# Sigmoids written as tanh, gate products in halves, head shares added one by one, and another order of work within a tick

## The chip, the cores and the metric

The kernel runs on one core of one Trainium2 chip. Its time is device microseconds of one launch; the median of three runs before the change is 3244.39 us (3243.58 to 3248.15). The engines are called TensorE (PE, with PEld for its weight loads), VectorE (DVE), ScalarE (ACT), GpSimd (POOL) and SyncE (SP, which issues most DMAs).

## The reference

A sequence of 512 tokens of width 1024 goes through two blocks, all in float32. The first block has two layers; each is a feed-forward network (width 2816), a mixer, a cross attention over 256 memory tokens, and a second feed-forward network. Layer 0 has the even mixer (eight heads of banded attention with sinks, eight heads of stick-breaking attention), layer 1 the odd mixer (16 heads of 64, three dilated bands in one softmax). The second block has a recurrent unit and a sparse attention side by side, then a feed-forward network:

```python
r = sigmoid(xb @ w_a + b_a); i = sigmoid(xb @ w_x + b_x)
log_a = -8 * r * softplus(-lam); a = exp(log_a)
u = sqrt(-expm1(2 * log_a)) * (i * x)          # h[t] = a[t] * h[t-1] + u[t]
merged = sigmoid(g_a) * y_a + sigmoid(g_b) * y_b
mix = merged @ w_o
```

`y_a` is the recurrent unit's output through a projection, `y_b` that of the attention (16 heads, 4 key-value heads, keys outside a query's 128 best by index scores are masked out).

## The kernel before, in words

Each float32 product is made of three matmuls of float32r parts: every operand is split into a high part (a rounded copy, ScalarE) and a low part (a subtraction, VectorE). Activations lie with features on the partitions, eight tiles of 128 x 512. `feat` (matmuls at L312 to L314) makes one 128 x 512 block of features in one PSUM bank by 24 matmuls; `tok_bank` (L785 to L787) makes token-major projections, two token tiles of 256 columns to a bank, 48 matmuls a bank. `weights` loads a weight block by SyncE's queue and splits it (L306 ScalarE, L307 VectorE). PSUM has 8 banks; SBUF temporaries are 36 slots of 128 x 512.

An attention pair is two heads (`heads`, which drives two `head` generators). Scores are 24 matmuls of 64 rows into six banks (L920); VectorE adds the bias and takes the maximum, which frees the bank (L944); ScalarE makes the exp and its sums (L953); GpSimd normalizes (L963); TensorE transposes the probabilities into three banks for each head (L974), which `evac` copies out in two parts (L848 ScalarE, L849 VectorE); eight matmuls multiply them with the values into one bank (L983, L984). The values' high and low parts sit side by side, so rows 0 to 63 and 64 to 127 of that bank are two shares of one head's result. `finish_heads` adds the shares of both heads when both are there (L993 and L994 copy, L995 and L996 add) and splits the sum (L514, L515).

What runs when is written as ticks. `drive` takes a list of ticks, each with fills (projections, output units, gates) and tasks (heads). All are generators, and every `yield` hands over to the next tick. In each tick `drive` starts the fills, then steps the generators that are under way, oldest first, then starts the tasks. This gives the order in which instructions are issued, which the compiler's scheduler takes as priority: on each engine an instruction of lower priority goes ahead where it reckons that the one of higher priority is not ready. The result is a fixed order on each engine. A pair takes five ticks: scores, maxima and exp of both heads; normalizing the first; transposes of the first and normalizing the second; values of the first and transposes of the second; values of the second. A new pair starts every second tick.

The odd mixer fills its ticks with query, key and value projections of four heads (`proj`, whose banks are held from the first half of its matmuls to the scaling three ticks later) and with the first output units. The second block's attention has query projections in every fourth tick and, in odd ticks, `gate_b`: a `feat` product, a scaling, a sigmoid and a store to DRAM. `merge_b` loads that back, multiplies it with the attention's projection, adds the recurrent side, and splits. Before this, the recurrent stage runs eight `rnn_block`s (two gate sigmoids, tanh, exp, square, square root, gelu, a scan) beside the index scores and the steps that find the 128 best keys on VectorE (L1542, L1543), and eight `merge_a` units with the other gate. ScalarE loads a table before a function that the loaded one lacks; the compiler places these loads, and in the profile they carry the line of the activation that follows.

Of the kernel before, what the change touches and what calls it, by code (L numbers as in the profile page):

```python
# [10 lines left out]
F32 = mybir.dt.float32  # L11
# [3 lines left out]
OP = mybir.AluOpType  # L15
# [159 lines left out]
class Net:  # L175
# [413 lines left out]
    def drive(self, ticks):  # L589
# [7 lines left out]
        def step(g, into):  # L597
            try:
                next(g)
                into.append(g)  # L600
            except StopIteration:
                pass

        i = 0
        while i < len(ticks) or act:
            fills, tasks = ticks[i] if i < len(ticks) else ((), ())
            i += 1
            new = []
            for f in fills:
                start(f, new)  # L610
            old = []
            for g in act:
                step(g, old)
            for f in tasks:
                start(f, new)
            act = old + new
# [286 lines left out]
    def heads(self, lay, q, k, biases, values, pair, sinks=(None, None)):  # L903
# [18 lines left out]
        one, two = (self.head(lay, order, sb[x], biases[x], values[x], pair, sinks[x]) for x in range(2))  # L922
# [4 lines left out]
        yield  # L927
        next(one)
        next(two)
        yield  # L930
# [5 lines left out]
    def head(self, lay, order, sb, bias, v, pair, sink):  # L936
# [43 lines left out]
        pair.append(po)  # L980
# [4 lines left out]
        self.put(ts)  # L985

    def finish_heads(self, one, two):


        nc = self.nc  # L990
# [152 lines left out]
    def stick(self, q, k, r0, v, pair):  # L1143
# [47 lines left out]
        pair.append(po)  # L1191
# [4 lines left out]
        self.put(s)  # L1196


    def odd_mixer(self, rms, w, wout):
# [37 lines left out]
        self.drive(ticks)  # L1237
# [313 lines left out]
    def rnn_consts(self):  # L1551
# [29 lines left out]
        v.tensor_scalar(self.c8, p, 8.0, None, OP.mult)  # L1581
        v.tensor_scalar(self.nc8, p, -8.0, None, OP.mult)
# [20 lines left out]
    def rnn_block(self, b, rms, w, gw, YH, YL):  # L1603
# [16 lines left out]
        for z, (o, bias) in enumerate(((r, "rg_b_a_2"), (i, "rg_b_x_2"))):  # L1620
# [16 lines left out]
        nc.scalar.activation(m, m, AF.Sqrt)  # L1637
# [167 lines left out]
    def second(self, out):  # L1805
# [28 lines left out]
        def merge_a(b):  # L1834
# [3 lines left out]
            nc.scalar.activation(t, t, AF.Sigmoid)  # L1838
# [3 lines left out]
            def finish(b, pa):  # L1842
                nc.vector.tensor_mul(t, t, pa)
# [208 lines left out]
```

## Time and profile before

| | before |
|---|---|
| median of 3 runs | 3244.39 us (3243.58 to 3248.15) |
| profiled execution | 3245.68 us, span 3243.9 us |
| TensorE, weight load | busy 3132.0 us (97%), 2819.2 us (87%) |
| VectorE | 2264.3 us (70%) |
| ScalarE | 1629.8 us (50%) |
| GpSimd | 358.0 us (11%) |
| mean granted clock of TensorE | 0.984 |
| the chain that ended last | PE 77%, DVE 12%, ACT 5%, issue 2%, DMA 2%, POOL 1% |

The span runs from the first to the last instruction on the core, and the time of the execution includes what lies around it. Busy time is the union of an engine's instructions; waiting, branching and issuing DMAs are not counted. The chain is followed back from the last instruction, at each step to what released it. In order of time the stages are: feed-forward, even mixer (about 350 to 626 us), cross attention, feed-forward twice, odd mixer (about 1490 to 1760 us), cross attention, feed-forward, then the second block from about 2300 us: the recurrent stage to about 2575, attention to about 2771, merging and output projection, feed-forward.

### The profile page before, as it was taken

To read this page: it belongs to the slowest core of one execution; us is meant where nothing else is said; L and a number is where in the kernel's file an instruction comes from. 1 tells how busy PE (TensorE), PEld (TensorE's weight loads), DVE (VectorE), ACT (ScalarE), POOL (GpSimd) and SP (SyncE) were. 2 spreads that over 40 slices of the span, in tenths; PEclk is the share of its full clock that TensorE was granted. 3 is DMA by queue.
4 is the path that set the end of the run, shared out by engine and by line. 5 is a ranking of instruction groups with operands and counts; after the bars stand their busy time and mean duration, and the time that the engine had idled before them with its cause. 6 is when DMAs were issued, how large, how long until landed. Compare 5 with 4: busy or idle time off the path is not lost.

```text
span 3243.9 us, 50967 instructions
## 1 busy us (share of the span) xinstructions
PE 3132.0 (97%) x20420; PEld 2819.2 (87%) x20420; DVE 2264.3 (70%) x3416; ACT 1629.8 (50%) x2711; POOL 358.0 (11%) x543
## 2 busy tenths in 40 slices
PE   8999999999999999999999999999999998989998
PEld 7999887798999999999887989999876887789997
DVE  8877566656777697775557557777689455478675
ACT  6544455655444364434556555443486277354444
POOL 1000123201000010001122010000222132210001
PEclk9999998999999999999999999999999999989999
DMA  4322211322233223322223322332312321513321
GB/s 158 109 97 85 94 50 56 121 96 84 93 101 98 96 95 111 100 76 88 85 72 111 117 79 75 111 101 76 105 60 91 104 79 47 168 53 105 105 91 65
DMA packets 104335, 300.81 MB, mean 93 GB/s; under 512 B 13857, under 2 KB 17441, under 8 KB 104097
## 3 DMA queue, kind: packets, MB, share of 16 engines
q1 hardware_dynamic: 94464, 287.74, 27.3%
q10 hardware_dynamic: 9632, 9.80, 1.0%
q8 instruction: 160, 2.62, 0.3%
q14 instruction: 79, 0.64, 0.1%
HBM read 291.21 MB, written 6.29 MB: 92 GB/s over the span
## 4 chain that ended last, share of the span: by engine, by line
PE 77%; DVE 12%; ACT 5%; issue 2%; DMA 2%; POOL 1%; ACTq 0%; SPq 0%; DVEq 0%; POOLq 0%
PE bank L312 19%; PE bank L313 18%; PE bank L314 18%; PE bank L787 4%; PE bank L785 4%; PE bank L786 4%; DVE wlo L307 2%; ACT whi L306 1%; PE bank L1765 1%; PE bank L1766 1%; PE bank L1767 1%; DVE wlo L428 1%; DVE slot L515 1%; DVE gl L578 1%; PE bank L974 1%
## 5 line engine op out<-in xcount | busy, mean ns | idle before, releaser
L312 PE MATMUL bank<-slot,whi 128*128 128x256 f32 (+1 forms) x2768 | 910.0, 330 | 16.7 <-ACT slot L514 9.6
L313 PE MATMUL bank<-slot,whi 128*128 128x256 f32 (+1 forms) x2768 | 911.8, 330 | 3.5 <-DVE slot L515 3.5
L314 PE MATMUL bank<-slot,wlo 128*128 128x256 f32 (+1 forms) x2768 | 911.1, 329 | 0.0
L427 ACT CAST whi<-fq 128x1024 fp32r<-128x1024 f32 x350 | 365.7, 1048 | 504.4 <-PE bank L313 409.7
L306 ACT CAST whi<-raw 128x1024 fp32r<-128x1024 f32 (+3 forms) x363 | 345.5, 954 | 521.3 <-PE bank L313 295.3
L312 PEld LDWEIGHTS bank<-slot,whi 128*128 128x128 f32 x2768 | 521.2, 188 | 70.5 <-ACT slot L514 12.3
L313 PEld LDWEIGHTS bank<-slot,whi 128*128 128x128 f32 x2768 | 521.8, 188 | 57.9 <-DVE slot L515 7.1
L314 PEld LDWEIGHTS bank<-slot,wlo 128*128 128x128 f32 x2768 | 523.0, 189 | 50.9
L307 DVE TENSOR_TENSOR wlo<-raw,whi 128x1024 fp32r<-128x1024 f32 (+3 forms) x363 | 411.8, 1136 | 218.8 <-ACT whi L306 218.0
L312 PE MATMUL bank<-gh,whi 128*128 128x256 f32 (+1 forms) x1712 | 538.8, 316 | 13.1 <-ACT whi L352 8.7
L314 PE MATMUL bank<-gh,wlo 128*128 128x256 f32 (+1 forms) x1712 | 534.7, 313 | 3.8 <-DVE wlo L353 2.5
L313 PE MATMUL bank<-gl,whi 128*128 128x256 f32 (+1 forms) x1712 | 535.5, 313 | 1.0 <-DVE gl L578 1.0
L428 DVE TENSOR_TENSOR wlo<-fq,whi 128x1024 fp32r<-128x1024 f32 x350 | 426.2, 1221 | 147.9 <-ACT whi L427 147.4
L312 PEld LDWEIGHTS bank<-gh,whi 128*128 128x128 f32 x1712 | 325.1, 190 | 39.8 <-ACT whi L352 9.4
L314 PEld LDWEIGHTS bank<-gh,wlo 128*128 128x128 f32 x1712 | 325.8, 190 | 26.0 <-DVE wlo L353 3.4
L313 PEld LDWEIGHTS bank<-gl,whi 128*128 128x128 f32 x1712 | 325.7, 190 | 24.0 <-DVE gl L578 2.3
L785 PE MATMUL bank<-whi,gh 128*128 128x256 f32 (+1 forms) x1056 | 303.7, 288 | 2.7 <-DVE slot L852 2.7
L787 PE MATMUL bank<-whi,gl 128*128 128x256 f32 (+1 forms) x1056 | 301.4, 286 | 1.5 <-DVE gl L578 1.5
L786 PE MATMUL bank<-wlo,gh 128*128 128x256 f32 (+1 forms) x1056 | 301.2, 285 | 1.1 <-DVE wlo L307 0.9
L172 POOL TENSOR_TENSOR sqacc<-sqacc,slot 128x512 f32<-128x512 f32 x62 | 100.5, 1621 | 1550.1 <-ACT slot L168 1549.2
L785 PEld LDWEIGHTS bank<-whi,gh 128*128 128x128 f32 x1056 | 202.5, 192 | 4.1 <-DVE slot L852 3.2
L786 PEld LDWEIGHTS bank<-wlo,gh 128*128 128x128 f32 x1056 | 202.6, 192 | 2.4 <-DVE wlo L307 2.0
(319 smaller groups left out, 4612.4 us busy)
## 6 DMA issues: line engine op xcount, KB each, us to landing
fq<-in_ffn_w_gu_dram SPq DMA_DIRECT2D x160, 512.0 KB, 3.3
raw<-in_ffn_w_down_dram SPq DMA_DIRECT2D x96, 384.0 KB, 3.1
raw<-in_w_in_dram SPq DMA_DIRECT2D x46, 512.0 KB, 3.4
raw<-in_xa_w_kv_dram SPq DMA_DIRECT2D x32, 512.0 KB, 3.5
raw<-in_od_w_in_dram SPq DMA_DIRECT2D x24, 512.0 KB, 3.3
raw<-in_w_ffn_down_dram SPq DMA_DIRECT2D x22, 512.0 KB, 3.5
fq<-in_w_ffn_gate_dram SPq DMA_DIRECT2D x40, 256.0 KB, 2.8
fq<-in_w_ffn_up_dram SPq DMA_DIRECT2D x40, 256.0 KB, 3.3
```

The lines of the kernel that those rows point to most:

```text
L172: self.net.nc.gpsimd.tensor_add(self.parts[0], self.parts[0], sq)
L306: nc.scalar.copy(hi[:, :n], raw[:, :n])
L307: nc.vector.tensor_sub(lo[:, :n], raw[:, :n], hi[:, :n].bitcast(F32))
L312: mm(ps, wh, xh, start=start, stop=False, **k)
L313: mm(ps, wh, xl, start=False, stop=False, **k)
L314: mm(ps, wl, xh, start=False, stop=stop, **k)
L427: self.nc.scalar.copy(hi[:, :n], t[:, :n])
L428: self.nc.vector.tensor_sub(lo[:, :n], t[:, :n], hi[:, :n].bitcast(F32))
L515: nc.vector.tensor_sub(lo, src, hi.bitcast(F32))
L785: mm(o, XH[k][:, t], wh, start=first, stop=False, skip_group_check=True)
L786: mm(o, XH[k][:, t], wl, start=False, stop=False, skip_group_check=True)
L787: mm(o, XL[k][:, t], wh, start=False, stop=last, skip_group_check=True)
```

## The change

Four things change. Sigmoids in the second block become tanh, by sigmoid(x) = (1 + tanh(x/2)) / 2, with the halves moved into constants and scales of instructions nearby; the product of input gate and convolution thereby goes from GpSimd to VectorE. `gate_b` gives way after half of its matmuls, and starts in even ticks. A head's shares are added right after its value matmuls, in attention pairs and in the stick-breaking heads. And in the odd mixer and the second block's attention `drive` goes through a tick in another order: first the steps under way that are not marked, then the tasks (scores), then the fills, last the marked steps. `heads` marks the steps that begin with transposes of the first head and with values of the first and transposes of the second.

```diff
-    def drive(self, ticks):
+    def drive(self, ticks, heads_first=False):
...
         def step(g, into):
             try:
-                next(g)
-                into.append(g)
+                into.append((g, next(g)))
             except StopIteration:
                 pass
...
-            new = []
-            for f in fills:
-                start(f, new)
-            old = []
-            for g in act:
-                step(g, old)
+            old, new = [], []
+            if not heads_first:
+                for f in fills:
+                    start(f, new)
+            for g, late in act:
+                if not (late and heads_first):
+                    step(g, old)
             for f in tasks:
                 start(f, new)
+            if heads_first:
+                for f in fills:
+                    start(f, new)
+                for g, late in act:
+                    if late:
+                        step(g, old)
             act = old + new
...
         next(one)
         next(two)
         yield
         next(one)
-        yield
+        yield True
         next(one)
         next(two)
-        yield
+        yield True
         next(one, None)
         next(two)
         yield
         next(two, None)
...
         po = self.bank()
-        pair.append(po)
...
         self.put(ts)
+        if x == 0:
+            pair.append(self.get())
+        self.add_halves(pair[0].f, po, x)
+
+    def add_halves(self, o, po, x):
+        here, there = slice(64 * x, 64 * x + 64), slice(64 - 64 * x, 128 - 64 * x)
+        self.nc.scalar.copy(o[here, :], po[there, :])
+        self.nc.vector.tensor_add(o[here, :], po[here, :], o[here, :])
...
-    def finish_heads(self, one, two):
-        t, h, l = self.get(3)
-        lo, hi = slice(0, 64), slice(64, 128)
-        nc.scalar.copy(t.f[lo, :], one[hi, :])
-        nc.scalar.copy(t.f[hi, :], two[lo, :])
-        nc.vector.tensor_add(t.f[lo, :], one[lo, :], t.f[lo, :])
-        nc.vector.tensor_add(t.f[hi, :], two[hi, :], t.f[hi, :])
+    def finish_heads(self, t):
+        h, l = self.get(2)
         self.split(h.r, l.r, t.f)
...
-        self.drive(ticks)
+        self.drive(ticks, True)
...
-            nc.scalar.activation(o, pg, AF.Sigmoid, bias=self.col(bias, b))
-        nc.gpsimd.tensor_mul(i, i, xc.f)
-        nc.scalar.activation(m, r, AF.Tanh, scale=self.c8[:, b:b + 1])
-        nc.scalar.activation(r, r, AF.Exp, scale=self.nc8[:, b:b + 1])
+            nc.scalar.activation(o, pg, AF.Tanh, bias=self.hb[z][:, b:b + 1], scale=0.5)
+        c8, nc8 = self.c8[:, b:b + 1], self.nc8[:, b:b + 1]
+        v.scalar_tensor_tensor(i, i, 1.0, xc.f, OP.add, OP.mult)
+        nc.scalar.activation(m, r, AF.Tanh, scale=c8, bias=c8)
+        nc.scalar.activation(r, r, AF.Exp, scale=nc8, bias=nc8)
...
-        nc.scalar.activation(m, m, AF.Sqrt)
+        nc.scalar.activation(m, m, AF.Sqrt, scale=0.25)
...
-            nc.scalar.activation(t, t, AF.Sigmoid)
+            nc.scalar.activation(t, t, AF.Tanh, scale=0.5)
...
-                nc.vector.tensor_mul(t, t, pa)
+                nc.vector.scalar_tensor_tensor(t, t, 1.0, pa, OP.add, OP.mult)
...
         def gate_b(b):
-            pg = self.feat(w[:, 5192 + b * P:5192 + (b + 1) * P], self.GH, self.GL)
+            wh, wl = self.weights(w[:, 5192 + b * P:5192 + (b + 1) * P], ND, P)
+            pg = self.bank()
+            for k in range(ND):
+                if k == ND // 2:
+                    yield
+                self.mm3(pg, wh[:, k, :], wl[:, k, :], self.GH[k], self.GL[k], k == 0, k == ND - 1)
             t = self.scratch()
             nc.vector.tensor_mul(t, pg, rms.R)
-            nc.scalar.activation(t, t, AF.Sigmoid)
+            nc.scalar.activation(t, t, AF.Tanh, scale=0.5)
...
-                self.split(h.r, l.r, t.f)
+                nc.scalar.mul(h.r, t.f, 0.5)
+                nc.vector.scalar_tensor_tensor(l.r, t.f, 0.5, h.r.bitcast(F32), OP.mult, OP.subtract)
...
-            x = [q(h // 4 + 1)] if h % 4 == 0 and h < 12 else [G(h // 2)] if h % 2 else []
-            ticks.append((x, [] if h % 2 else [H(h // 2)]))
-        self.drive(ticks + [([B(0)], []), ([B(1)], [])])
+            x = [q(h // 4 + 1)] if h % 4 == 0 and h < 12 else []
+            ticks.append((x + ([] if h % 2 else [G(h // 2)]), [] if h % 2 else [H(h // 2)]))
+        self.drive(ticks + [([B(0)], []), ([B(1)], [])], True)
```

Left out above: the same call of `add_halves` at the end of `stick`, and in `rnn_consts` the factors 8 and -8, which become 4 and -4, and the two gate biases times 0.5 (`hb`, 128 x 8 each).

## Rows read from the trace of the kernel before

**Rows 1.** The page's head: span, then TensorE's busy us, share, instructions.
```profile
span 3243.9 us, 50967 instructions
PE 3132.0 (97%) x20420; PEld 2819.2 (87%) x20420; DVE 2264.3 (70%) x3416; ACT 1629.8 (50%) x2711; POOL 358.0 (11%) x543
```

**Rows 2.** Windows: length, busy (instructions) of PE, PEld, DVE, ACT, POOL; PEclk, DMA, GB/s.
```profile
350.00:626.00 276.00, 264.10 (x1560) 224.71 (x1559) 177.93 (x330) 157.14 (x321) 66.62 (x110) 0.96 0.23 78
1561.00:1755.00 194.00, 176.56 (x1272) 161.34 (x1272) 117.14 (x294) 103.84 (x258) 40.85 (x100) 0.96 0.21 66
2300.00:2575.00 275.00, 262.92 (x1310) 215.32 (x1308) 205.03 (x355) 157.85 (x209) 57.00 (x80) 0.98 0.28 91
2600.00:2771.00 171.00, 154.11 (x989) 133.96 (x987) 99.74 (x260) 118.33 (x256) 49.25 (x100) 0.96 0.19 63
...
2695.00:2702.00 7.00, 6.56 (x39) 6.46 (x40) 3.60 (x6) 3.67 (x8) 0.76 (x3) 0.76 0.20 76
...
1563.00:1575.00 12.00, 9.00 (x50) 8.43 (x49) 7.11 (x25) 5.55 (x20) 5.68 (x15) 0.72 0.38 133
```

**Rows 3.** Waits of TensorE, 2575 to 2800 us: total us, times, longest.
```profile
PE bank L983 <- ACT slot L848: 11.8, 4, 4.0
PE bank L920 <- DVE slot L849: 4.5, 8, 1.2
```

**Rows 4.** Timeline of ScalarE from 2692.78 us: start, us, instruction.
```profile
2692.78 0.19 ACT L953 ACTIVATION_READ_ACCUMULATOR slot<-slot,nm 128x1 f32 x1
2692.99 1.28 ACT L1918 ACT_TABLE_LOAD   x1
...
2694.82 1.33 ACT L848 CAST slot<-bank 128x512 fp32r<-128x512 f32 x3
```

**Rows 5.** Timeline of TensorE at the same place; idle time and releaser in brackets.
```profile
2691.69 1.28 PE L974 MATMUL bank<-ident,slot 128*128 128x128 f32 x10
2695.44 0.51 PE L983 MATMUL bank<-slot,vv 128*128 128x512 f32 x1 [2.47 <-ACT slot L848]
```

**Rows 6.** Groups by line, ScalarE, 2575 to 2771 us: busy, mean ns, idle before.
```profile
L953 ACT ACT_TABLE_LOAD x8 | 10.3, 1283 | 10.3 <-DVE nm L947 10.3
L1918 ACT ACT_TABLE_LOAD x8 | 10.3, 1283 | 0.1
```

**Rows 7.** Waits of TensorE, 1490 to 1760 us.
```profile
PE bank L920 <- DVE mx L944: 4.6, 2, 2.9
PE bank L920 <- DVE slot L849: 3.6, 3, 1.5
...
PE bank L312 <- ACT slot L514: 1.4, 1, 1.4
```

**Rows 8.** Timeline of TensorE in the odd mixer, at a later pair's scores.
```profile
1610.77 1.32 PE L920 MATMUL bank<-slot,slot 64*128 64x512 f32 x6
1613.22 2.63 PE L920 MATMUL bank<-slot,slot 64*128 64x384 f32 x18 [1.14 <-DVE slot L849]
```

**Rows 9.** Timeline of ScalarE and of VectorE at the end of a pair, odd mixer.
```profile
1745.60 0.58 ACT L994 COPY slot<-bank 64x512 f32<-64x512 f32 x1 [1.15 <-PE bank L984]
...
1746.21 0.69 DVE L996 TENSOR_TENSOR slot<-bank,slot 64x512 f32<-64x512 f32 x1 [0.89 <-ACT slot L994]
```

**Rows 10.** Waits of TensorE, 350 to 626 us.
```profile
PE bank L312 <- ACT slot L514: 2.8, 2, 1.8
```

**Rows 11.** Recurrent stage: a wait of TensorE, a window, two groups by line.
```profile
PE bank L312 <- POOL slot L512: 6.4, 3, 3.2
...
2450.00:2475.00 25.00, 24.32 (x103) 19.04 (x103) 25.00 (x49) 22.18 (x26) 9.38 (x7) 1.00 0.24 71
...
L1635 DVE SCALAR_TENSOR_TENSOR rn<-slot,rn 128x512 f32<-128x512 f32 x8 | 5.4, 680 | 0.0
...
L1628 ACT ACT_TABLE_LOAD x8 | 10.3, 1283 | 0.1
```

More of the change, by code (lines that the diff above doesn't have):

```diff
@@ L921, in heads @@
                        skip_group_check=True)
-        one, two = (self.head(lay, order, sb[x], biases[x], values[x], pair, sinks[x]) for x in range(2))
+        one, two = (self.head(lay, order, sb[x], biases[x], values[x], pair, sinks[x], x) for x in range(2))
         next(one)
@@ L934, in heads, with head @@
         next(two, None)
-    def head(self, lay, order, sb, bias, v, pair, sink):
+    def head(self, lay, order, sb, bias, v, pair, sink, x):
         nc = self.nc
@@ L985, in head @@
         self.put(ts)
-    def finish_heads(self, one, two):
-        nc = self.nc
-        t, h, l = self.get(3)
-        lo, hi = slice(0, 64), slice(64, 128)
-        nc.scalar.copy(t.f[lo, :], one[hi, :])
-        nc.scalar.copy(t.f[hi, :], two[lo, :])
-        nc.vector.tensor_add(t.f[lo, :], one[lo, :], t.f[lo, :])
-        nc.vector.tensor_add(t.f[hi, :], two[hi, :], t.f[hi, :])
+        if x == 0:
[7 more added lines that the diff above has]
+        h, l = self.get(2)
         self.split(h.r, l.r, t.f)
@@ L1190, in stick @@
         po = self.bank()
-        pair.append(po)
         for j, (b, off, q0, w) in enumerate(K):
@@ L1196, in stick @@
         self.put(s)
+        if r0 == 0:
+            pair.append(self.get())
+        self.add_halves(pair[0].f, po, r0 // 64)
     def odd_mixer(self, rms, w, wout):
@@ L1580, in rnn_consts @@
         self.nc8 = m
-        v.tensor_scalar(self.c8, p, 8.0, None, OP.mult)
-        v.tensor_scalar(self.nc8, p, -8.0, None, OP.mult)
+        v.tensor_scalar(self.c8, p, 4.0, None, OP.mult)
+        v.tensor_scalar(self.nc8, p, -4.0, None, OP.mult)
+        self.hb = []
+        for t, name in ((e, "rg_b_a_2"), (l, "rg_b_x_2")):
+            v.tensor_scalar(t, self.pv[:, ROWS[name][0]:ROWS[name][0] + n], 0.5, None, OP.mult)
+            self.hb.append(t)
     def gate_weights(self):
@@ L1619, in rnn_block @@
         r, i, m = t1[:, 0:512], t1[:, 512:1024], t1[:, 1024:1536]
-        for z, (o, bias) in enumerate(((r, "rg_b_a_2"), (i, "rg_b_x_2"))):
+        for z, o in enumerate((r, i)):
             wh, wl = gw[z]
@@ L1926, in finish @@
             def finish(b, pa):
-                nc.vector.tensor_mul(t.f, t.f, pa)
+                nc.vector.scalar_tensor_tensor(t.f, t.f, 1.0, pa, OP.add, OP.mult)
                 nc.gpsimd.tensor_add(t.f, t.f, m.f)
                 h, l = self.get(2)
-                self.split(h.r, l.r, t.f)
+                nc.scalar.mul(h.r, t.f, 0.5)
+                nc.vector.scalar_tensor_tensor(l.r, t.f, 0.5, h.r.bitcast(F32), OP.mult, OP.subtract)
                 self.put(t, m)
```

## The prediction

> **What bounds the kernel now.** I read the page's head first: TensorE is busy 97% of the span [rows 1]. A change that removes no matmul can give back only TensorE's idle time and the time it spends at the lower of its two clock levels (1.2 against 2.4 GHz). So the second view is busy time by stage [rows 2]: of 276 us of the even mixer TensorE idles 11.9, of 194 us of the odd mixer 17.4, of 275 us of the recurrent stage 12.1, and of 171 us of the second block's attention 16.9. The granted clock in the same rows turns into lost time by (1 - clock) x length: 0.96 in both attention stages is 7.8 us (odd) and 6.8 us (second). Everything the change can win lies in these sums, some 49 us in the two attention stages.
>
> Third, what ends the idle time. In the second block's attention it is nearly two waits: the probability-times-value matmuls for ScalarE's copy of the transposed probabilities (11.8 us in 4 waits), and the scores for VectorE's half of the same eviction, that is, for PSUM banks (4.5 us in 8) [rows 3]. In the odd mixer the scores again wait for banks, held by the maxima (4.6 us in 2) or by an eviction (3.6 in 3) [rows 7].
>
> **The change part by part.** All sums are against the profiled execution, 3245.7 us (span 3243.9, 1.8 around it); the median of the runs shown is 3244.4, 1.3 lower, which I take off at the end.
>
> *Sigmoid to tanh in the second block's attention.* The four long waits have one picture: the last exp ends at 2692.97, a table load of 1.28 us for the gate's sigmoid starts at 2692.99, then the sigmoid runs, and only then the three copies at 2694.82 [rows 4]; TensorE's transposes end at 2692.97 and the next matmul starts at 2695.44, 2.47 us idle [rows 5]. There are 8 loads at the sigmoid and 8 at the exp that follows [rows 6]; the exp's load lies on the way from scores to transposes, which has at least a tick of other work beside it, so only the sigmoid's, right before copies that TensorE waits for, counts. If tanh needs no load beside exp, each wait loses 1.28 us: 4 x 1.28 = 5.1 us. The bounds are 0 (tanh evicts exp's table as sigmoid does) and 5.1. I take 5.1: in the recurrent block the tanh follows the sigmoid without a load of its own in all 8 blocks, while sigmoid, exp, square root and gelu each have one (8 at the exp, and rows like it with 7, 8 and 8) [rows 11], so tanh is the one function there that never causes a load.
> That row doesn't show tanh and exp in one table, though. The Trainium skill (ScalarE: Activation LUTs, "Table sets: the hidden batching unit") states it: the set whose main function is exp also holds tanh. By that the 5.1 stands; no row here can show it. The same page of the Trainium skill ("What ACT_TABLE_LOAD costs") prices a switch at about 2.66 us, a 1.28 us load and a drain of 1.38 us. The row differs: the load starts 0.02 us after the exp's last piece, and nothing but the 1.28 us is lost. By the Trainium skill's price four switches would be 10.6 us and the time some 5.5 us lower than mine; the measurement decides.
>
> *Scores first, transposes last, gates in halves (second block).* Of the 11.8 us, 6.7 are left. They arise where the second head's transposes are followed at once by the products that need their eviction. Now half a gate product (12 of 24 matmuls) lies in each tick, and a query projection's second half and the next pair's scores are at hand. No row shows the new order; bounds are 0 and all 6.7, and I take half, 3.4, as the new order still puts that second product right behind the transposes, at the head of the next tick. The scores' wait of 4.5 us: scores now follow that product and not the first head's transposes. Bounds 0 and 4.5, half is 2.2. Splitting the gate costs no matmul; it holds one bank and one weight buffer a tick longer. Clock: around one of the long waits the granted clock is 0.76 over 7 us, 1.7 us lost [rows 2], a quarter of the stage's 6.8, so I put the other three quarters at the other three waits. Bounds 0 and 6.8, half is 3.4. Stage: 5.1 + 3.4 + 2.2 + 3.4 = 14.1 us less.
>
> *The same order in the odd mixer.* Projections keep their two banks over several ticks there. The scores' waits are 8.2 us [rows 7]; 2.9 of these belong to the first pair, which has no older pair to be put before, so its order stays. A later one shows the mechanism: six score matmuls start on free banks at 1610.77, the other 18 at 1613.22, 1.14 us of it idle [rows 8]. In the new order the scores follow the other head's transposes, with the same three banks to be drained, but with all fills behind them in the tick. Bounds 0 and 5.3; half is 2.7. Clock: 7.8 us, of which 3.4 lie beside the first pair's wait (0.72 over 12 us [rows 2]); of the other 4.4 half, 2.2.
>
> *Shares added at once.* The number of copies and adds is unchanged, 64 x 512 each, but at the end of a pair one copy (0.58 us) and one add (0.69) [rows 9] are already done: the chain to the split is 1.27 shorter. It ends a wait in the odd mixer (1.4 us, one [rows 7]), which falls by 1.3, and two in the even mixer (1.8 and 1.0 us [rows 10]), which fall by 1.3 and 1.0. Bounds 0 and 3.6; the full 3.6 is taken, because the wait is directly on this chain. The bank of the first head also comes free a tick earlier; I price that at nothing, since even-mixer waits aren't on banks. Odd mixer: 2.7 + 2.2 + 1.3 = 6.2; even mixer 2.3.
>
> *Recurrent block.* ScalarE loses about one load in four per block (tanh after gelu or exp), some 10 us; the longest waits there don't end on it but on GpSimd's split at the end of a block's chain (6.4 us in 3) [rows 11], behind a VectorE that is busy 25.00 of 25 us [rows 11]. And VectorE gets the product of input gate and convolution from GpSimd, 8 x 0.68 = 5.4 us by a like instruction [rows 11]. If a third of the blocks fall in the saturated stretch, it is some 2 us later there, against a load of 1.28 less ahead of the last square root. Bounds: 6.4 gained, 5.4 lost; I take 0. If VectorE's cover of other work is gone, the 5.4 is exposed, with the clock falling as it already does behind that wait.
>
> *The rest.* Factors of one half move into instructions that exist anyway (scalar operands of the same passes); two 128 x 8 products are added in a stage where they lie beside matmuls: 0.
>
> Sum: 14.1 + 6.2 + 2.3 + 0 = 22.6. 3245.7 - 22.6 - 1.3 = 3221.8, say 3222.
>
> **The rivals.**
> *Slower: transposes, then their product, then scores, with nothing between.* By the written order the second head's transposes end an odd tick, and the next tick opens with that head's product, which needs their eviction, and with scores, which need six of eight banks while three are being drained. The row prices it: 2.45 us from the end of the transposes to free banks (1610.77 to 1613.22) [rows 8], plus 1.7 of low clock. Seven such places a stage make 29.1 us: second block 29.1 - 23.7 = +5.4; odd mixer 29.1 + 2.9 + 3.4 - 25.2 = +10.2; less 3.6 for the shares: +12.0, 3256. It decides once TensorE has no ready fill at that place in most pairs. For it: the odd mixer's projections hold two to four banks. Against: in the second block every other even tick has the second half of a query projection at hand, and part of the scores fits in the free banks.
> *The order moves the waits and wins nothing.* Then loads and shares are left: 5.1 + 3.6 = 8.7, 3236. For it: the bank count is unchanged. Against: the scores start a projection earlier.
> *All of it fits.* Both attention stages run without idle time but for the first pair: 16.9 + 6.8 + 14.5 + 4.4 + 2.3 = 44.9, 3199. For it: the stages have enough projections. Against: the first pair's 2.9 us shows how the banks bind even with projections at hand.
> *The loads stay*, because exp and tanh lie in different tables after all: 22.6 - 5.1 = 17.5, 3227. For it: the exp that follows a tanh has a load in all 8 recurrent blocks [rows 11]. Against: the table then loaded is the sigmoid's, so the row doesn't say what another one holds.
>
> **How the numbers follow.** Chances: forecast 0.50 (own range 3211 to 3233), order wins nothing 0.20, all fits 0.13, slower 0.12, loads stay 0.05. A measurement here tells 0.2%, 6.5 us, from no change. The faster side (below 3238) gets 0.49 + 0.12 + 0.13 + 0.04 = 0.78, no change 0.13 (part of the second case, the tails of the others), slower 0.09. The range 3199 to 3251 takes in the unknown terms from nearly all gained to 5.4 lost; outside are most of the slower case and half of the case in which all fits, some 0.15.
>
> **What would show it.** Right: no table load between the gates and the exps of the second block's attention but at its start; the wait for the transposed copies there from 11.8 to about 3 us; the granted clock of that stage at 0.98; the end-of-pair split waits in both mixers gone; the recurrent stage as long as before. Wrong: loads still 8 and 8; product or score waits of over 2 us in most pairs; the odd mixer's idle time not below 17 us; the recurrent stage longer by 5 us, on VectorE.

## The result, and the profile after

The changed kernel takes 3264.41 us (median of 6 runs, 3258.88 to 3269.23), the kernel before beside it 3246.42 (6 runs): a ratio of 1.0052, 95% interval 1.0038 to 1.0066. (Ratios here and below are those on record with their intervals; the quotient of the two medians can differ from them by up to 0.1%.) It is slower by half a per cent, where 3222 us were forecast and the range ended at 3251. The profiled execution took 3263.85 us.

The head of the page, kernel after. Against [rows 1], TensorE is busy 11.4 us more for the same 20420 instructions; its mean granted clock fell from 0.984 to 0.980, so this is time at the lower clock level:
```profile
span 3262.1 us, 50959 instructions
PE 3143.4 (96%) x20420; PEld 2824.9 (87%) x20420; DVE 2265.0 (69%) x3426; ACT 1600.4 (49%) x2686; POOL 343.1 (11%) x535
```
The windows by stage of the kernel after (columns as in [rows 2]): even mixer, odd mixer from first score to last value product, recurrent stage, second block's attention likewise.
```profile
350.00:626.00 276.00, 266.56 (x1567) 226.41 (x1566) 177.79 (x329) 156.89 (x320) 65.04 (x110) 0.95 0.23 77
1562.00:1764.00 202.00, 178.11 (x1272) 160.93 (x1272) 117.78 (x294) 104.72 (x257) 40.64 (x99) 0.94 0.19 63
2308.00:2583.00 275.00, 264.53 (x1321) 217.61 (x1321) 208.30 (x374) 148.87 (x202) 52.55 (x87) 0.98 0.30 95
2603.00:2791.00 188.00, 170.36 (x1032) 145.09 (x1032) 101.18 (x265) 98.84 (x243) 45.67 (x100) 0.92 0.19 62
```
The odd mixer idles 23.9 us of 202 (17.4 of 194 in [rows 2]). The second attention idles 17.6 of 188, about what it did, but its clock fell from 0.96 to 0.92: (1 - 0.92) x 188 = 15.0 us lost against 6.8.

To compare runs I measure between marks: in the odd mixer from the first matmul of the token norm before it to that of the norm behind it ("odd"), in the second block from the first key projection to the first matmul of the next norm ("second"). "Second" holds the same 1692 matmuls in every kernel. "Odd" doesn't: where the odd mixer's fills stand behind the scores, 96 projection matmuls lie ahead of its first mark, elsewhere 144, so about 5 us of the same work fall inside "odd" in six of the kernels (marked *) and outside it in the others. The column "odd + ff" therefore starts at the norm before the feed-forward ahead of the odd mixer; it holds the same 4358 matmuls in every kernel, and what the order costs the odd mixer is read from it. "Span" is from the first score to the last value product in it; idle is its length less TensorE's busy time, clock is (1 - granted clock) x length. In us, one profiled execution each:

| kernel | odd | odd + ff | span / idle / clock | second | span / idle / clock | ratio to before |
|---|---|---|---|---|---|---|
| before | 291.6 | 642.7 | 193.0 / 17.4 / 8.5 | 293.8 | 169.6 / 16.5 / 6.8 | 1 |
| after | 305.3* | 652.2 | 201.5 / 23.9 / 11.9 | 302.5 | 187.5 / 17.2 / 15.4 | 1.0052 |
| old order in both | 288.7 | 640.0 | 190.6 / 15.7 / 8.5 | 285.9 | 159.2 / 7.1 / 5.1 | 0.9945 |
| old order in odd | 292.8 | 644.0 | 192.4 / 17.4 / 8.5 | 306.5 | 190.7 / 15.1 / 22.2 | 1.0009 |
| old order in second | 308.7* | 655.2 | 203.4 / 22.5 / 15.4 | 283.2 | 159.1 / 7.0 / 5.1 | 0.9980 |
| q/k banks freed at once | 322.3* | 668.4 | 217.3 / 29.3 / 25.6 | 302.5 | 187.0 / 16.8 / 15.4 | 1.0082 |
| exponentials behind | 308.9* | 655.1 | 203.2 / 21.1 / 17.1 | 280.7 | 166.8 / 8.9 / 0.0 | 0.9998 |
| scores first only | 296.2* | 642.2 | 189.9 / 16.2 / 10.2 | 279.0 | 161.2 / 8.1 / 0.0 | 0.9945 |
| transposes last only | 304.3 | 655.1 | 205.5 / 28.5 / 13.7 | 316.8 | 191.0 / 33.6 / 17.1 | 1.0092 |
| bias early | 298.4* | 644.8 | 194.4 / 18.2 / 10.2 | 300.7 | 185.2 / 17.3 / 11.9 | 1.0008 |
| before + tanh | 295.5 | 646.1 | 194.2 / 15.8 / 13.7 | 282.4 | 157.8 / 7.5 / 3.4 | 0.9957 |
| before + shares | 290.3 | 641.3 | 191.5 / 17.1 / 8.5 | 294.2 | 170.5 / 18.3 / 8.5 | 0.9992 |
| before + gate halves | 290.1 | 641.2 | 191.7 / 17.3 / 6.8 | 289.8 | 163.7 / 10.1 / 6.8 | 0.9997 |
| the best combination | 290.5 | 641.8 | 189.8 / 15.6 / 8.5 | 279.4 | 161.2 / 8.2 / 0.0 | 0.9928 |

How far such a stretch can be trusted: the even mixer, whose code is the same in "after" and the nine kernels made from it, measures from 272.0 to 278.9 us in them. Differences under some 5 us in one execution are therefore left to the timed ratios. Nor is the profiled execution always a middling one: it is the slowest of its kernel's runs for the three kernels with an old order, scores first only and before + tanh, and the fastest for exponentials behind. From before to after "odd + ff" is 9.5 us longer, second 8.7, even mixer 2.3 (275.5 to 277.8), the stage behind the last norm 1.3, the recurrent stage 0.7 shorter: 21.1, of which the unchanged rest gives back 2.9 in this execution, to the 18.2 by which the span grew.

**The odd mixer.** TensorE's waits from 1555 to 1765 us, kernel after. The scores' waits for banks of [rows 7] (4.6 and 3.6 us) are down to 2.4 and some small ones; in their place the next projection (L793) waits for the first maximum, a wait that is not among the seven largest there before:
```profile
PE bank L793 <- DVE mx L952: 10.4, 4, 2.9
PE bank L990 <- ACT slot L856: 4.2, 5, 2.2
PE bank L312 <- ACT slot L514: 2.7, 2, 1.8
PE bank L928 <- DVE mx L952: 2.4, 1, 2.4
```
One of the four, in a timeline of all engines, kernel after (ACTq and SP issue DMAs):
```profile
1604.92 0.58 ACT L1000 COPY slot<-bank 64x512 f32<-64x512 f32 x1 [2.25 <-PE bank L991]
1605.53 0.69 DVE L1001 TENSOR_TENSOR slot<-bank,slot 64x512 f32<-64x512 f32 x1 [2.01 <-ACT slot L1000]
1606.26 0.62 ACT L514 CAST slot<-slot 128x512 fp32r<-128x512 f32 x1 [0.76 <-DVE slot L1001]
1606.27 0.82 ACTq L1129 DMA_DIRECT2D slot<-in_c_bias_o_dram  x2
1606.28 0.61 PE L928 MATMUL bank<-slot,slot 64*128 64x256 f32 x5 [0.57 <-DVE slot L1001]
...
1609.01 0.69 DVE L952 CUSTOM_DVE_ANT_0 slot<-bank,slot 128x512 f32<-128x512 f32 x1 [1.41 <-DMA slot<-in_c_bias_o_dram]
...
1609.76 0.58 PE L793 MATMUL bank<-whi,gh 128*128 128x256 f32 x1 [2.87 <-DVE mx L952]
```
Read it as a chain. The new pair's bias tiles are loaded by ScalarE's queue, and their issue stands there behind the split that ends the previous pair. That split waits for the add, the add for the copy, the copy for the previous pair's last value product. Now the scores run directly behind that product, so they are done (1606.89) before the bias has landed. The first maximum needs the bias, starts at 1609.01, frees the first bank at 1609.70, and the projection starts. In the old order the tick's projection stands ahead of the scores.

**The second attention.** TensorE's waits from 2590 to 2790 us, kernel after; against [rows 3] (11.8 us in 4 waits of up to 4.0) the same wait is now 14.1 in 10 of up to 2.0, while the scores' waits for banks (4.5 us in 8) are down to 1.4 in 2:
```profile
PE bank L990 <- ACT slot L856: 14.1, 10, 2.0
PE bank L991 <- DVE slot L857: 2.8, 7, 0.8
```
ScalarE's and then TensorE's timeline at one of them, kernel after:
```profile
2629.87 0.72 ACT L961 ACTIVATE slot<-slot,nm 128x512 f32<-128x512 f32 x1 [3.32 <-DVE nm L955]
...
2634.16 0.19 ACT L961 ACTIVATION_READ_ACCUMULATOR slot<-slot,nm 128x1 f32 x1
2634.25 1.05 ACT L856 CAST slot<-bank 128x512 fp32r<-128x512 f32 x2
```
```profile
2629.69 1.25 PE L982 MATMUL bank<-ident,slot 128*128 128x128 f32 x10
...
2633.35 0.39 PE L314 MATMUL bank<-gh,wlo 128*128 128x512 f32 x1
2634.87 0.50 PE L990 MATMUL bank<-slot,vv 128*128 128x512 f32 x1 [1.12 <-ACT slot L856]
```
The transposes are done at 2630.9, and half a gate product covers their eviction until 2633.7. But the copies stand in ScalarE's queue behind the eight exponentials of the new pair, which were issued with its scores earlier in the tick and so have priority: 4.38 us, 2629.87 to 2634.25. No table load is in the way any more; exponentials and tanh run one after the other without one.

### The profile page after: what moved, and what is told of

It is laid out like the page before. It is cut to its first block, busy times and chain, and to the rows that moved or that the text cites. A ratio compares the mean times of both kernels' runs of the same rounds, so it can differ in the third digit from the quotient of the medians.

```text
span 3262.1 us, 50959 instructions
## 1 busy us (share of the span) xinstructions
PE 3143.4 (96%) x20420; PEld 2824.9 (87%) x20420; DVE 2265.0 (69%) x3426; ACT 1600.4 (49%) x2686; POOL 343.1 (11%) x535
## 4 chain that ended last, share of the span: by engine, by line
PE 80%; DVE 10%; ACT 5%; DMA 2%; issue 2%; POOL 1%; ACTq 0%; SPq 0%; DVEq 0%; POOLq 0%
PE bank L312 19%; PE bank L313 19%; PE bank L314 19%; PE bank L793 4%; PE bank L795 4%; PE bank L794 4%; DVE wlo L307 2%; PE bank L1782 1%; PE bank L1783 1%; PE bank L1784 1%; ACT slot L961 1%; ACT whi L306 1%; PE bank L991 1%; DVE wlo L428 1%; PE bank L982 1%
## 5 line engine op out<-in xcount | busy, mean ns | idle before, releaser
L312 PE MATMUL bank<-slot,whi 128*128 128x256 f32 (+1 forms) x2768 | 909.0, 330 | 17.2 <-ACT slot L514 7.7
L306 ACT CAST whi<-raw 128x1024 fp32r<-128x1024 f32 (+3 forms) x363 | 345.5, 953 | 527.6 <-PE bank L313 295.5
L793 PE MATMUL bank<-whi,gh 128*128 128x256 f32 (+1 forms) x1056 | 306.4, 290 | 10.4 <-DVE mx L952 10.4
L794 PE MATMUL bank<-wlo,gh 128*128 128x256 f32 (+1 forms) x1056 | 302.5, 287 | 0.0
L793 PEld LDWEIGHTS bank<-whi,gh 128*128 128x128 f32 x1056 | 204.5, 194 | 12.7 <-DVE mx L952 11.5
L795 PEld LDWEIGHTS bank<-whi,gl 128*128 128x128 f32 x1056 | 204.1, 193 | 2.1 <-DVE gl L578 2.1
```

The costliest lines, as they stand in the source:

```text
L306: nc.scalar.copy(hi[:, :n], raw[:, :n])
L312: mm(ps, wh, xh, start=start, stop=False, **k)
L793: mm(o, XH[k][:, t], wh, start=first, stop=False, skip_group_check=True)
L794: mm(o, XH[k][:, t], wl, start=False, stop=False, skip_group_check=True)
L795: mm(o, XL[k][:, t], wh, start=False, stop=last, skip_group_check=True)
```

## The experiments

My theory after the result: the new order costs what the rest gains. The rival: the rest gains nothing, or costs.

**1. The old order.** All of the change but the order.
```diff
-        self.drive(ticks, True)          # odd mixer
+        self.drive(ticks)
-        self.drive(ticks + [([B(0)], []), ([B(1)], [])], True)   # second block
+        self.drive(ticks + [([B(0)], []), ([B(1)], [])])
```


> The changed kernel with the old order of a tick in both attention stages; tanh, shares at once and gate halves stay. Theory A (the new order alone costs: in the odd mixer a projection waits for a bank behind the scores, in the second block the new pair's exps stand ahead of the eviction copies on ScalarE): both stages get their old waits back less the table loads, so 5 to 12 us less than the kernel before (0.9963 to 0.9985 of it), and TensorE's wait of a projection for the maxima (10.4 us in the odd mixer of the changed kernel) is gone. Rival B (the halves of the gate or the earlier share adds cost, by a bank held longer and small copies in ScalarE's queue): still 8 us or more above the kernel before, with the second block's attention as long as in the changed kernel (187 us from first score to last value product).


Measured: 3232.53 us, ratio 0.9945 (0.9927 to 0.9963). The order alone turns a gain of 0.55% into a loss of 0.52%; theory A holds, and the rest gains more than the 0.37% that it allowed at most. Waits of the second attention in this kernel:
```profile
PE bank L928 <- DVE slot L857: 5.1, 10, 1.0
PE bank L990 <- ACT slot L856: 1.2, 3, 0.6
```

**2 and 3. The old order in one block at a time.** One of the two lines above each.


> The changed kernel with the old order in the odd mixer only. Theory A: the odd mixer takes back its 13.7 us (305 us from norm to norm falls to 288 to 293), the second block's attention stays at 187 us, and the whole is some 5 us above the kernel before (1.0005 to 1.0030). Rival B (the shares cost in the odd mixer as well): the odd mixer stays above 298 us.

> The changed kernel with the old order in the second block's attention only. Theory A: the odd mixer stays at 305 us, the attention from first score to last value product falls from 187 to 165 to 172 us (with one projection less to do there than in the changed kernel's 187, whose stage before the first score is 6 us shorter), and the whole is within 6 us of the kernel before, on either side. Rival B (gate halves cost): attention stays above 178 us.


Measured: old order in the odd mixer 3252.04 us, 1.0009 (0.9996 to 1.0023); in the second block 3241.41, 0.9980 (0.9968 to 0.9992). From after's 1.0052 these take back 14 and 23 us; both together took 35. The loss lies in both blocks, more of it in the second. In the profiles the odd mixer came back as expected (292.8 us); the second attention was shorter than expected with its old order (159.1 us) and, where it kept the new one, longer (190.7), at a clock loss of 22.2 us in place of 15.4.

**4. Banks freed at once in the odd mixer.** The earlier query or key projection still holds two of eight banks when the six for scores are taken. Here its scaling (squares, root, product) is issued at once, and the transposes behind it keep their tick.
```diff
-            al = yield from self.heads_alpha(banks, rms.y, 4, 64, 256, NT)
+            al = self.at_once(self.heads_alpha(banks, rms.y, 4, 64, 256, NT))   # runs it to its end
             tm = [self.heads_scale(...)]
             yield
+            yield
+            yield
```


> The changed kernel, but the odd mixer's query and key projections are scaled out of their banks in the tick of their second half instead of two ticks later; transposes stay in their tick. Theory A1 (after the 24 score matmuls all eight banks are taken, six by scores and two by the earlier projection, so the next projection waits for the first maximum): the wait of a projection for the maxima falls from 10.4 us in 4 to under 3 us, and the odd mixer from 305 to 290 to 297 us. Rival A2 (VectorE is simply late with the maxima because the eviction of the transposes stands ahead of them, banks or not): the waits stay at 2 us or more each.


Measured: 3274.48 us, 1.0082 (1.0063 to 1.0101), so the expectation missed. The projections' wait for maxima is gone, as it should be with two more banks; but the scaling now stands ahead of other things in the queues of VectorE and ScalarE. At the first of its long waits for copies, ScalarE idles 2.04 us for GpSimd before the scaling's two small steps at 1600.84, and the copies behind them start at 1601.93, 2.4 us after their transposes. Waits in its odd mixer:
```profile
PE bank L998 <- ACT slot L864: 9.8, 6, 3.0
PE bank L793 <- DVE slot L857: 8.8, 2, 4.4
```
In this kernel the spreading over ticks, which looks like waste in the bank count, keeps those queues free.

**5. Exponentials behind the transposes' copies.** This aims at ScalarE's queue alone: maxima stay with the scores, the exponentials are issued at the end of the tick.
```diff
+        yield                                # in head, between maxima and exponentials
...
         next(one)
         next(two)
+        if self.behind is None:              # in heads; a list where the new order is on
+            next(one)
+            next(two)
+        else:
+            self.behind += [one, two]        # drive runs these behind the marked steps
```


> The changed kernel, in which the exponentials of a new pair are issued at the end of the tick, behind the transposes and their evictions, instead of straight behind the maxima. Theory A (in the second attention the copies of the transposes queue on ScalarE behind 16 exponentials, so the value products wait): the PE wait of the value products for ScalarE there falls from 14.1 us to under 5, the stretch from the first score to the last value product from 187.5 to 165-177 us, the whole to 3248-3256 us. In the odd mixer the waits of projections for the first maxima (10.4 us) stay, and its stretch is within 6 us of 201.5. Rival B (the loss is the clock of TensorE, because transposes and value products stand together with nothing between): the stretch stays at 183-190 us with a clock loss of 13 us or more, and the whole at 3260-3268 us.


Measured: 3243.46 us, 0.9998 (0.9984 to 1.0011), by the ratios some 17 us below the changed kernel. The second attention falls from 302.5 to 280.7, its span to 166.8, and its clock loss to nothing. The wait and ScalarE's timeline at the like place:
```profile
PE bank L1000 <- ACT slot L860: 6.1, 6, 2.7
```
```profile
2628.06 0.19 ACT L971 ACTIVATION_READ_ACCUMULATOR slot<-slot,nm 128x1 f32 x1
2628.16 0.56 ACT L860 CAST slot<-bank 128x512 fp32r<-128x512 f32 x1
2628.62 0.73 ACT L971 ACTIVATE slot<-slot,nm 128x512 f32<-128x512 f32 x1
```
The exponentials now have the lower priority, and the scheduler places copies between them: the first copy starts 1.2 us after the end of the transposes (2627.01 to 2628.16), where it took 3.3 in the changed kernel (2630.94 to 2634.25). The wait fell to 6.1 us, not below 5; the time came out below what theory A said. The odd mixer did not gain (203.2 against 201.5), so its cause is another. Rival B, that the clock is lost whatever ScalarE does, falls: the clock came back with the wait.

**6 and 7. The two halves of the order.** Scores first only: the two marks are taken away, so transposes and products run at the head of the tick.
```diff
-        yield True
+        yield
```
Transposes last only: the marks stay, and the projections go back to the front.
```diff
-            if not heads_first:
+            if True:                              # fills ahead of all
                 for f in fills:
                     start(f, new)
...
             if heads_first:
-                for f in fills:
-                    start(f, new)
                 for g, late in act:
```


> The changed kernel with the two marks taken away: in a tick the old steps (transposes and value products with them) come first, then the scores, then the projections. Theory A (two separate mechanisms: in the odd mixer scores ahead of projections cost the banks, in the second attention transposes behind the new exponentials cost ScalarE's queue): odd mixer still 197-204 us from first score to last value product, with 6 us or more of projections waiting for maxima; second attention 158-172 us, with the value products' wait for ScalarE under 5 us; whole 3242-3254 us. Rival B (the late transposes do the harm in both blocks): odd 188-193 us as well, whole 3230-3240 us. Rival C (scores ahead of projections do it in both): both stretches stay within 4 us of 201.5 and 187.5, whole 3258-3268 us.

> The changed kernel with the projections put back to the front of a tick; the transposes and the value products behind the scores stay last. Theory A: odd mixer without waits of projections for maxima (under 2 us of the 10.4), 190-196 us from first score to last value product; second attention still 182-190 us, with 10 us or more of value products waiting for ScalarE; whole 3248-3258 us. Rival B (late transposes do the harm in both blocks): odd stays at 198-205 us too, whole 3260 us or more. Rival C (scores ahead of projections do it in both): both fall, second to 158-170 us, whole 3228-3240 us.


Measured: scores first only 3227.43 us, 0.9945 (0.9931 to 0.9960), as good as the old order; transposes last only 3276.73, 1.0092 (1.0075 to 1.0109), worse than both together. Rival B held in both: it is the late transposes that cost, in both blocks (odd + ff 640.0 and 642.2 us without them, 655.1 and 652.2 with them, with the fills ahead of the scores and behind). Scores ahead of the fills cost nothing that shows, and with late transposes they even take back 0.4%. I had given the odd mixer's wait to scores ahead of projections; with that order and no late transposes it is nearly gone (waits of scores first only, odd mixer):
```profile
PE bank L793 <- DVE mx L952: 1.6, 2, 1.5
```
There a head's transposes run between the previous pair's end and the scores, and VectorE's maxima wait 1.1 us for bias loads in all (6.0 in the changed kernel). The second attention of transposes last only has the copies behind the exponentials, as the changed kernel has, and waits longer for them:
```profile
PE bank L988 <- ACT slot L854: 25.5, 7, 3.8
PE bank L980 <- DVE mx L950: 7.8, 7, 1.5
```

**8 to 10. The other parts alone**, each on the kernel before: the sigmoids as tanh; the shares added head by head; the gate products in halves and in even ticks (the diffs are those parts of the change).


> The kernel before with only the sigmoids as tanh. If the table loads between exponential and sigmoid in the second attention were what the path lost there: the 16 loads of that stretch go, its length from first score to last value product falls from 169.6 to 160-165 us, and the whole by 4-9 us (ratio 0.9972-0.9988). Rival (the loads were hidden and another wait ends last): the loads go and the stretch stays within 2 us, ratio 0.9993-1.0007. The recurrent part is expected unchanged within 2 us in both.

> The kernel before with only the shares added at once, head by head, instead of at the end of a pair. If the wait of the split for the adds (2.8 us in the even mixer, 1.4 in the odd) is shortened: ratio 0.9985-0.9995. If, as the changed kernel's trace has it, those waits do not shorten: 0.9995-1.0007. If what the old order gained without it (18 us with all three parts) lies here, by banks that come free earlier: under 0.998.

> The kernel before with only the gate products of the second attention in halves, started in the even ticks. Work spread between the head steps: the second attention from first score to last value product falls from 169.6 to 160-167 us, waits of the value products for the copies (4.5 us) and the clock loss (6.8 us) shrink, ratio 0.9972-0.9992. Rival (the gates only change places, and the table loads still stand before the copies): within 2 us, ratio 0.9994-1.0008.


Measured: tanh 3233.38 us, 0.9957 (0.9941 to 0.9973); shares 3245.18, 0.9992 (0.9981 to 1.0003); gate halves 3246.50, 0.9997 (0.9987 to 1.0006). Tanh gains 14 us (9 to 19 by the interval) where 4 to 9 were expected; the other two can't be told from nothing. Waits of the second attention, with tanh alone and with gate halves alone (value products for ScalarE's copies; 11.8 in 4 before [rows 3]):
```profile
PE bank L983 <- ACT slot L848: 1.0, 1, 1.0
```
```profile
PE bank L983 <- ACT slot L848: 1.4, 1, 1.4
```
Either part alone takes nearly the whole wait away, so together they have little more to win (old order in the second block: 285.9 and 283.2 in two kernels, tanh alone 282.4). But the wait that went is not yet time. With gate halves alone the scores wait longer for banks (6.8 us in 10, and 1.2 more for an add, against 4.5 in 8), so that only 6.4 us of idle time go, the stage is 4.0 us shorter, and the timed ratio shows nothing.

**11. The bias early.** The changed kernel, with the two bias tiles of a pair loaded one tick earlier in the odd mixer.
```diff
-            bt = [self.vbias(a["c_bias_o"][2 * p + x], 512) for x in range(2)]   # in heads(p)
+            bt = st["bt", p]
...
+        for p in range(1, 8):
+            ticks[4 + 2 * p][0].append(lambda p=p: load(p))    # load(0) likewise in tick 4
```


> The changed kernel; in the odd mixer the two bias tiles of a pair are loaded one tick earlier, so that their load no longer stands on ScalarE's queue behind the previous pair's last split. Theory A (with the scores first and the transposes last, the scores stand alone behind the previous pair's value products, and the first maximum, which frees the first bank, waits for the bias to land: issue at 1606.27, first maximum at 1609.01 us): the PE waits of projections for maxima fall from 10.4 us to under 4, the odd mixer from norm to norm from 305.3 to 292-299 us, the whole to 3250-3258 us. Rival B (too few free banks, whatever the bias does): 7 us or more of those waits stay and the odd mixer keeps 301-308 us. The second attention is untouched (302.5 us within 4) in both.


Measured: 3249.16 us, 1.0008 (0.9998 to 1.0019): some 14 us of the loss back, more than the 7.4 that its odd mixer shows in the profile (odd + ff 644.8 against 652.2; the even mixer, the same code, is 5.4 shorter in this execution). The whole came out just below theory A's 3250 to 3258 us. The wait fell between the two bounds:
```profile
PE bank L793 <- DVE mx L952: 5.9, 4, 1.6
```
```profile
1592.68 0.82 ACTq L1129 DMA_DIRECT2D slot<-in_c_bias_o_dram  x2
...
1602.02 0.69 DVE L952 CUSTOM_DVE_ANT_0 slot<-bank,slot 128x512 f32<-128x512 f32 x1
...
1602.77 0.38 PE L793 MATMUL bank<-whi,gh 128*128 128x256 f32 x1 [1.49 <-DVE mx L952]
```
(the wait list, then a timeline at the place that 1609.01 was before). The first maximum no longer waits for a load and starts 0.74 us after the scores end (1601.28); what is left, 1.49 instead of 2.87 us, is that maximum itself and VectorE's split ahead of it. So both theories hold in part: 4.5 of the 10.4 us were the bias, 5.9 come from scores that stand directly before a projection with no bank free. Against the old order in both the stage is still 4.8 us longer (odd + ff 640.0), which one execution can't tell; by the timed ratio the early bias gives back as much as the old order in the odd mixer does (1.0008 and 1.0009). Why so much, with 5.9 us of waits left, is not shown.

**12. The best combination.** Tanh, halves and shares; odd mixer in the old order with the bias early; second attention with scores first and no marks.
```diff
-        yield True
+        yield                       # both marks
-        self.drive(ticks, True)     # odd mixer alone
+        self.drive(ticks)           # with the loads of experiment 11
```


> What the runs so far point to: tanh, halves and shares of the change; the odd mixer in the old order with its bias loads one tick early; the second attention with scores first but no step put last. From the stretches of the earlier runs: odd mixer 288.6 us norm to norm less 2-6 us for the waits of scores for first maxima that the early bias takes away (5.2 us there), second attention 276 us from the first key projection to the norm, against 291.5 and 293.8 before: 20-24 us less in all, ratio 0.9920-0.9942. Rival (the early loads only move the wait to the next bank, and the second attention's 276 us do not hold beside another odd mixer): 0.9943-0.9960.


Measured: 3223.65 us, 0.9928 (0.9916 to 0.9941), 22.7 us below the kernel before and faster than both kernels. The whole came out in the middle of what was expected, its parts did not. The second attention is 279.4 us, as in experiment 6 (279.0), where 276 were expected. The early bias gained nothing: odd is 290.5 us (288.7 with the old order alone) where 283 to 287 were expected. VectorE's wait for the load went (3.0 us in 2 with the old order, none now), but the scores wait 3.7 us for maxima as they did without it (3.9): in that order it was not the load that TensorE waited for. The two stages give 15.3 of the 21.8 us by which the span is shorter than before; the rest lies in code that didn't change or can't be told from it. Its even mixer is at the low end of its spread (272.0), so the lead over experiments 1 and 6 (0.9945) is not certain.
```profile
span 3222.1 us, 50967 instructions
PE 3124.4 (97%) x20420; PEld 2811.7 (87%) x20420; DVE 2262.6 (70%) x3426; ACT 1600.2 (50%) x2686; POOL 343.5 (11%) x535
```

## Why the prediction was wrong, step by step

**The order in the second attention: forecast -9.0 us (copies 3.4, scores' banks 2.2, clock 3.4), measured +16.6** (285.9 with the old order to 302.5). This is the step that failed first. The forecast bounded each term by zero and by all of the old wait, as if the new order could only help, and followed TensorE's order alone. It named the half gate products that would cover the copies, and they do lie there; it did not ask what stands ahead of the copies on ScalarE. Moving scores ahead of the transposes moves their eight exponentials and eight reads of sums ahead of the copies. Experiment 5, which lowers the exponentials alone, brings the stage back to 280.7 us. The scores' wait for banks did go, as forecast, and paid nothing. The clock was forecast to cost half of its 6.8 us and cost 15.4; with the exponentials behind it cost nothing. By the timed ratios the order costs this block some 23 us.

**The order in the odd mixer: forecast -4.9 us (banks 2.7, clock 2.2), measured +12.2** (odd + ff 640.0 to 652.2; 14 by the timed ratios). The forecast counted "all fills behind them in the tick" as cover for the scores. The place of the fills turned out not to matter alone (experiments 6 and 7). What failed is that the step moved last was put at no cost: the transposes had stood between a pair's end and the next scores, and had covered two things there, the bias load, which the scores' step issues on ScalarE's queue and which the prediction doesn't mention, and the maxima that free banks. Scores first alone costs nearly no such wait (1.6 us); with the transposes last it is 10.4, of which the early bias took 4.5. The prediction had named the sign: idle time of the odd mixer not below 17 us; it is 23.9.

**Table loads: forecast -5.1 us, measured -11.4 for the stage** (293.8 to 282.4 with tanh alone; idle 9.0 and clock 3.4 less in the span). The mechanism was right, and all 16 loads are gone. By the Trainium skill (ScalarE: Activation LUTs, "Table sets: the hidden batching unit") exp's set holds tanh too; the trace agrees, with 16 loads before and none after in that stage. What was mis-sized is the claim that only the sigmoid's load lies on the path. A timeline of ScalarE before, at the third of the four long waits, shows why:
```profile
2710.62 1.28 ACT L953 ACT_TABLE_LOAD   x1 [3.35 <-DVE nm L947]
2711.92 0.72 ACT L953 ACTIVATE slot<-slot,nm 128x512 f32<-128x512 f32 x1
```
Here and at the fourth wait the load for the exponentials starts only once their maxima are there, so they, the sigmoid's load and the copies behind are all later by it: two loads, 2 x 1.28 = 2.57 us, and with tanh the waits there fell from 2.80 to 0.09 and from 4.05 to 0.97. [rows 6] had it: the exponentials' loads have 10.3 us of idle time before them, ended by VectorE's nm (at three of the eight). At the first two of the four waits the load came early, while the maxima were still missing: only one load lay in the chain, and the waits still fell from 2.46 and 2.47 to 0.07. There TensorE's gate product before takes 7.4 us instead of 5.87, so part of the wait turned into lower clock.

**Shares: forecast -3.6 us, measured -2.6** (0.9992, that is -6.2 to +1.0): not settled. The waits that were to go did not: with the change the even mixer's is 2.3 us in 2 (2.8 in 2 before), the odd mixer's 2.7 in 2 (1.4 in 1).

**Gate halves:** no term of their own; alone they take the copies' wait from 11.8 to 1.4 us, and the time stays (0.9997). The forecast's 3.4 us for the copies were for order and halves together; by the interval the halves alone are worth 4.2 us at most.

**Recurrent block: forecast 0, measured -0.7** (231.6 to 230.9 us, single executions; 229.2 with tanh alone, and 227.6 to 233.8 in all kernels with tanh). Right as far as such spreads tell: 25 loads in place of 34 in that stretch, 9 x 1.28 = 11.5 us of ScalarE, shorten it by nothing like that.

**The rival that was slower** had the sign and the place in the second block (products right behind transposes), and got 0.12. Its mechanism was TensorE's banks at 2.45 us a place; what came was ScalarE's queue, 1.4 us at each of ten places (14.1 / 10), and in the odd mixer a wait behind the scores and not before them.

## What to carry to other kernels

When a step is moved ahead on one engine, list what it issues on every other queue, DMAs included, and what is then behind these: here eight exponentials with their sums, and in the odd mixer a small load, undid what the rest of the change won. A bound of zero for a reordering is a bound only once the waits that the old place had covered are named. Where two parts remove the same wait (tanh alone 11.8 to 1.0 us, gate halves alone 11.8 to 1.4), add their gains once, and ask which wait takes its place: the gate halves' 10.4 us gave no time that could be measured. And before two kernels are compared between two marks, count the instructions between them.

## What the runs showed of the hardware

TensorE's idle time and the time lost to the lower clock level stood in no fixed proportion. In the second attention 17.2 us idle in waits of up to 2.0 us went with 15.4 us of clock loss (kernel after), 16.5 us mostly in four waits of 2.5 to 4.0 with 6.8 (before), 33.6 with 17.1 (transposes last only), 7.1 with 5.1 (old order in both), and 8.9 with none (exponentials behind). In the changed kernel the lower level begins 0.9 us after each of two waits in succession (waits that end at 2679.75 and 2686.55 us, the lower level from 2680.6 and 2687.4). With the exponentials behind, a wait of 2.73 us that ends at 2750.33 has none after it. What decides between these is not shown. And unchanged code does not always get the same clock: the even mixer lost between 10.2 and 18.8 us to it in kernels that differ only elsewhere.
